# The down projection as seven products per block pair in three parts, its activations stored with their sums, and the weight sums added by GpSimd

## The chip, the core and the metric

The kernel runs on one core of a Trainium2 chip. The core has a matrix engine (TensorE, PE in the tables, with its weight loads as PEld), three engines for elementwise work (VectorE = DVE, ScalarE = ACT, GpSimd = POOL) and a queue engine that only issues transfers (SyncE = SP). Each engine works through its own list of instructions in order and waits at an instruction until the semaphores that it names are set. Sixteen DMA engines move data between the chip's DRAM and the on-chip memory (SBUF); TensorE's results land in PSUM. The metric is the device time of one execution in microseconds (us), lower is better.

## The reference, cut to what matters

One layer of an encoder in float32: an input projection, two attention branches, a gated merge with an output projection, and a convolutional GLU. The change lies in the GLU, and there in its last matrix product above all:

```python
SEQ, D_MODEL, D_FF = 512, 2048, 5632
h2 = rmsnorm(x, norm_ffn)
u  = h2 @ w_up                                   # (512, 2048) @ (2048, 11264)
u  = up[:, :-2]*cw[0] + up[:, 1:-1]*cw[1] + up[:, 2:]*cw[2] + conv_b   # up: u padded by one token
gate, val = jnp.split(u, 2, axis=-1)             # 5632 columns each
x  = x + (jax.nn.silu(gate) * val) @ w_down      # (512, 5632) @ (5632, 2048)
```

## The kernel before, in words

All matrices are held transposed (features on the 128 partitions, the 512 tokens along the free axis). A float32 product is made from three passes: every operand is split into a rounded half `hi` (a cast by ACT) and the rest `lo` (a subtraction by DVE), and hi·hi + hi·lo + lo·hi are summed in PSUM. All TensorE work goes through the helper `mm` (L77), and every SP transfer through `dma` (L74).

The program is a list of steps, run one after the other: attention and gates, the output projection (`project_out`), 22 slices of the up projection (`up`), and the down projection (`down`). A plain step takes weight units of 1024 columns in all (`Plain`: L154 is the cast, L155 the subtraction) and issues 24 matmuls of 128x512 for each.

The up projection is not a plain product. `products` computes a 512x512 block of the result from 2x2 blocks with seven block products in place of eight (Strassen's method in Winograd's form). For this the weights and the activations of a pair of 128-row blocks enter as seven matrices each: four blocks or their sums. A unit there is a `Product`: SP loads four weight blocks of 128x256 (`load`), three added operations make the four sums (`sums`, L573, L576, L577, all on DVE), and `prep` casts and subtracts them in two pieces, of 1024 and 768 columns (L596, L597). TensorE then issues 7 x 2 x 3 = 42 matmuls of 128x256. After the eight products of a slice, `combine` joins the seven PSUM banks into the two results (`u`); four of its DVE operations read PSUM. The activations' seven forms are made once (`forms`).

Each slice ends in a queue of eight entries, one run after each of the next eight products: scale by the row factor (L852), the convolution (`Conv`: ACT makes the three weighted copies, L865, L867, L873, and GpSimd's queue issues two accumulating DMAs for each of gate and val, L868, L875), SiLU (L887), the product with the gate (L890) and the store of the slice's two 128-row blocks to DRAM (`act`, L891, GpSimd's queue).

The order around the change: while TensorE runs product i, `advance` prepares product i+2, forms the sums of product i+3 and loads product i+5. `keep` pins an instruction to its written place on its engine; the rest is placed by the scheduler. For part of the products (in the middle slices the numbers 2, 3 and 7, in the first and last slice all eight; 76 in all) the sums are made much earlier, during gates and `project_out` (`make_early`), stored to DRAM by GpSimd's queue (`sums`, L580), and loaded again in place of the fourth block.

The down projection is plain: two parts of 11 slices each, in each part four steps of 512 output features, 22 units per step: 88 units, 2112 matmuls of 128x512. Its activations are read back from `act` and split once per part (`load_act`, `split_act`, L921, L922). The first part's results are added to x (`total`) in DRAM, the second's to that, and go out (L945, L950).

Of the kernel before, what the change touches and what calls it, by code (L numbers as in the profile page):

```python
# [38 lines left out]
def trunk_kernel(  # L39
# [14 lines left out]
    wst_ctx, att_ctx, f_ctx = ExitStack(), ExitStack(), ExitStack()  # L54
# [117 lines left out]
    def advance(*between):  # L172
# [7 lines left out]
        make_early()  # L180
# [363 lines left out]
    ffn, products_, early, made = {}, [], deque(), deque()  # L544
    keep = tc.keep_in_program_order

    class Product:
# [5 lines left out]
        def __init__(self, w, first, kept, turn):  # L553
            self.w, self.first, self.turn = w, first, turn
            self.kept = dram.tile([P, 4, 256], F32, name=f"sums{first}") if kept else None
            self.made = False

        def ready(self, phase, n):
            return "f" in ffn and not early and self.first <= n

        def load(self):
            f = self.f = ffn["f"].tile([P, 7, 256], F32, tag="f", name="f", bufs=4)
            dma(f[:, 0:2], self.w[:, :, 0])
            dma(f[:, 2], self.w[:, 1, 1])
            if self.made:
                dma(f[:, 3:], self.kept)
            else:
                dma(f[:, 6], self.w[:, 0, 1])

        def sums(self):  # L570
            if not self.made:
                f = self.f
                keep(nc.vector.tensor_tensor(  # L573
                    f[:, 3:5], f[:, 2::-2], f[:, 6].unsqueeze(1).to_broadcast([P, 2, 256]),
                    ALU.add))
                keep(nc.vector.tensor_tensor(f[:, 5], f[:, 4], f[:, 2], ALU.add))  # L576
                keep(nc.vector.tensor_tensor(f[:, 6], f[:, 5], f[:, 1], ALU.add))  # L577

        def store(self):
            nc.gpsimd.dma_start(self.kept, self.f[:, 3:])  # L580
            self.made = True
# [20 lines left out]
    def make_early():  # L602


        if "f" not in ffn or not early:
            return
        made.append(0)
        if len(made) % 5 == 0:
            return
        n = len(made) - len(made) // 5 - 1  # L610
        for move, i in (("store", n - 2), ("sums", n - 1), ("load", n)):
            if 0 <= i < len(early):
                getattr(early[i], move)()
        if n - 2 == len(early) - 1:
            early.clear()

# [3 lines left out]
    def forms(src):  # L620
# [4 lines left out]
        nc.vector.tensor_tensor(  # L625
# [401 lines left out]
```

## Time and profile before

| | |
|---|---|
| time, three runs | 2525.92 us median (2524.97 to 2532.28) |
| profiled execution | 2526.16 us; its span on the core 2524.4 us |
| granted TensorE clock | 0.999 |
| busy: PE, DVE, ACT, POOL | 2510.1, 1514.3, 1120.3, 205.8 us |
| up projection, 1195 to 2040 us | PE 843.6 of 845 us, DVE 683.5, ACT 537.5, POOL 112.0 |
| down projection, 2040 us to the end | PE 480.5 of 484.4 us, DVE 157.6, ACT 120.4, POOL 11.4 |
| read from and written to DRAM | 347.9 and 68.2 MB |

The page of the profile sums each engine's busy time over the span. The chain of waits follows the end of the execution back, at each point to what released the instruction. The view by windows gives the same sums for a stretch of time, with the count of instructions in brackets, the granted clock, the DMA share and GB/s. The timeline lists instructions by start and length (in us); "x2" are two in a row, counted as one stretch, and consecutive operations overlap a little at their ends. In the tables by form a row ends in busy time and mean ns of one.

### The profile page before, as it was taken

The page shows a single profiled execution, that of the slowest core. Times are in us where ns is not written, and L with a number is a line of the kernel's source. Part 1 is how long each engine was busy: PE and PEld are TensorE (multiplying, and loading weights), DVE is VectorE, ACT ScalarE, POOL GpSimd, SP SyncE. Part 2 cuts the span into 40 slices and gives each one's busy share as a digit, 9 for nine tenths or more (in the row PEclk, how much of TensorE's full clock was granted, in tenths as well). Part 3 has the DMA queues.
Part 4 walks back from the last instruction along what each step waited for, and adds up shares of the span by engine and source line. Part 5 has one row for each costly group of instructions (what it writes and reads, how often), then busy time and mean ns, then how long its engine had stood idle before and what let it go on. Part 6 is the DMA issues. An engine that isn't in the chain of part 4 may idle for free.

```text
span 2524.4 us, 38263 instructions
## 1 busy us (share of the span) xinstructions
PE 2510.1 (99%) x15016; PEld 2233.5 (88%) x15016; DVE 1514.3 (60%) x2155; ACT 1120.3 (44%) x1613; POOL 205.8 (8%) x248
## 2 busy tenths in 40 slices
PE   9999999999999999999999999999999999999999
PEld 7888888888888888888999999999999988888887
DVE  6566554635545457646788888888887762243222
ACT  5355544533122232325566666666666662132211
POOL 0100000000000000100011111111111110000000
PEclk9999999999999999999999999999999999999999
DMA  5323232337877887965578788787787895464443
GB/s 189 98 79 92 89 95 90 98 90 242 255 251 248 259 280 242 302 209 169 164 205 222 201 207 213 208 216 203 211 217 204 239 259 167 127 224 132 127 136 106
DMA packets 294677, 464.67 MB, mean 184 GB/s; under 512 B 23136, under 2 KB 190688, under 8 KB 294496
## 3 DMA queue, kind: packets, MB, share of 16 engines
q1 hardware_dynamic: 249408, 348.00, 44.3%
q0 software_dynamic: 40480, 105.83, 16.5%
q10 hardware_dynamic: 4608, 8.39, 0.9%
q8 instruction: 117, 1.92, 0.3%
q14 instruction: 64, 0.52, 0.1%
HBM read 347.93 MB, written 68.16 MB: 165 GB/s over the span
## 4 chain that ended last, share of the span: by engine, by line
PE 97%; DMA 2%; ACT 1%; DVE 0%; issue 0%; SPq 0%; ACTq 0%; DVEq 0%; POOLq 0%
PE mm L77 93%; PE tr L77 2%; PE tr L476 1%; DMA o<-a 1%; DMA s<-act 0%; PE tr L334 0%; ACT wh L596 0%; DMA f<-sums 0%; DVE wl L597 0%; PE tr L383 0%; DMA f<-in_w_up 0%; DMA raw<-in_w_in 0%; ACT s L632 0%; ACT t L248 0%; SPq L74 0%
## 5 line engine op out<-in xcount | busy, mean ns | idle before, releaser
L77 PE MATMUL mm<-s,hi 128*128 128x512 f32 x3712 | 1106.2, 390 | 0.9 <-DVE s L714 0.9
L77 PEld LDWEIGHTS mm<-s,hi 128*128 128x128 f32 x3712 | 695.9, 188 | 144.0 <-ACT s L715 1.3
L77 PE MATMUL mm<-s,wh 128*128 128x256 f32 x4928 | 807.0, 277 | 2.8 <-ACT wh L596 2.5
L155 DVE TENSOR_TENSOR lo<-raw,hi 128x1024 fp32r<-128x1024 f32 (+1 forms) x289 | 352.6, 1220 | 675.1 <-ACT hi L154 663.2
L77 PEld LDWEIGHTS mm<-s,wh 128*128 128x128 f32 x4928 | 701.0, 188 | 3.5 <-ACT wh L596 2.9
L154 ACT CAST hi<-raw 128x1024 fp32r<-128x1024 f32 (+1 forms) x289 | 303.5, 1050 | 879.5 <-PE mm L77 810.6
L77 PE MATMUL mm<-s,lo 128*128 128x512 f32 x1856 | 681.8, 390 | 0.0
L77 PE MATMUL mm<-s,wl 128*128 128x256 f32 x2464 | 583.6, 277 | 1.1 <-DVE wl L597 1.1
L597 DVE TENSOR_TENSOR wl<-f,wh 128x1024 fp32r<-128x1024 f32 x352 | 372.2, 1087 | 141.4 <-ACT wh L596 139.5
L596 ACT CAST wh<-f 128x1024 fp32r<-128x1024 f32 x352 | 317.7, 940 | 281.4 <-PE mm L77 255.0
L77 PEld LDWEIGHTS mm<-s,wl 128*128 128x128 f32 x2464 | 419.0, 188 | 1.5 <-DVE wl L597 1.5
L77 PEld LDWEIGHTS mm<-s,lo 128*128 128x128 f32 x1856 | 348.5, 188 | 71.5
L77 PE MATMUL mm<-hi,s 128*128 128x512 f32 x896 | 285.0, 394 | 5.6 <-ACT hi L154 5.6
L77 PEld LDWEIGHTS mm<-hi,s 128*128 128x128 f32 x896 | 167.8, 189 | 38.4 <-ACT hi L154 5.6
L77 PE MATMUL mm<-lo,s 128*128 128x512 f32 x448 | 176.3, 395 | 0.0
L573 DVE TENSOR_TENSOR f<-f 128x512 f32<-128x512 f32 x176 | 120.4, 684 | 0.0
L77 PEld LDWEIGHTS mm<-lo,s 128*128 128x128 f32 x448 | 84.6, 189 | 16.8
L580 POOL DMA_DIRECT2D sums<-f x76 | 40.6, 534 | 570.2 <-DVE f L577 570.2
L577 DVE TENSOR_TENSOR f<-f 128x256 f32<-128x256 f32 x176 | 74.6, 424 | 5.5
L576 DVE TENSOR_TENSOR f<-f 128x256 f32<-128x256 f32 x176 | 74.6, 424 | 5.3
L875 POOL DMA_DIRECT2D o<-a x44 | 52.6, 1197 | 304.4 <-ACT wh L596 152.0
L865 ACT ACTIVATE o<-u,smalls 128x512 f32<-128x512 f32 x88 | 71.2, 809 | 7.0 <-DVE o L890 4.0
(134 smaller groups left out, 1454.9 us busy)
## 6 DMA issues: line engine op xcount, KB each, us to landing
f<-in_w_up SPq DMA_DIRECT2D x252, 256.0 KB, 3.5
f<-in_w_up SPq DMA_DIRECT2D x428, 128.0 KB, 3.9
raw<-in_w_in SPq DMA_DIRECT2D x103, 512.0 KB, 3.8
raw<-in_w_down SPq DMA_DIRECT2D x88, 512.0 KB, 4.2
o<-a POOLq DMA_DIRECT2D x88, 511.0 KB, 6.2
sums<-f POOLq DMA_DIRECT2D x76, 512.0 KB, 5.1
f<-sums SPq DMA_DIRECT2D x76, 512.0 KB, 5.8
raw<-in_w_in SPq DMA_DIRECT2D x66, 256.0 KB, 3.0
```

What stands on the lines that cost most here:

```text
L77: nc.tensor.matmul(o, l, r, start=start, stop=stop, skip_group_check=True)
L154: nc.scalar.copy(hi[:, c:c + n], self.raw[:, c:c + n])
L155: nc.vector.tensor_tensor(lo[:, c:c + n], self.raw[:, c:c + n], hi[:, c:c + n].bitcast(F32), ALU.subtract)
L476: nc.tensor.transpose(b[:, (j - j0) * P:(j - j0 + 1) * P], pr[j][:, off:off + P], ident)
L573: keep(nc.vector.tensor_tensor(f[:, 3:5], f[:, 2::-2], f[:, 6].unsqueeze(1).to_broadcast([P, 2, 256]), ALU.add))
L576: keep(nc.vector.tensor_tensor(f[:, 5], f[:, 4], f[:, 2], ALU.add))
L577: keep(nc.vector.tensor_tensor(f[:, 6], f[:, 5], f[:, 1], ALU.add))
L580: nc.gpsimd.dma_start(self.kept, self.f[:, 3:])
L596: keep(nc.scalar.copy(hi, f))
L597: keep(nc.vector.tensor_tensor(lo, f, hi.bitcast(F32), ALU.subtract))
L865: keep(nc.scalar.activation(self.o[:, m], u[:, m], AF.Identity, bias=cb[:, i:i + 1], scale=cw[:, i, 1:2]))
L875: nc.gpsimd.dma_start(self.o[:, :, :S - 1], third[:, :, 1:], accum_op=ALU.add)
```

## The change

- `down` uses `products` as `up` does: seven block products per pair of 256 input features. The 22 pairs are taken in three parts of 7, 7 and 8, four steps each. That is 88 products of 42 matmuls of 128x256, 3696 in all.
- `up` makes the three activation sums before it stores (`form_sums`, three DVE operations per slice) and stores eight blocks of 128x256 instead of four, from SP's queue and one queue entry later. The last accumulating DMA of the gate is issued three entries later than before. `down` loads seven of the blocks per pair, and splits them.
- The DRAM copies of weight sums are gone. Each product's sums are made when it is used: by GpSimd in four additions of 128x256, except two of eight products (0 and 5) in slices after the first, and one or two per step in `down`, which stay on DVE with three additions.
- The results of the first two parts are added to `total` by accumulating DMAs from GpSimd's queue; in the third part DVE adds `total`, and the output leaves in two transfers of 512 KB per step.

```diff
-        def ready(self, phase, n):
-            return "f" in ffn and not early and self.first <= n
+        def ready(self, phase, n):
+            return "f" in ffn and self.first <= n
         def load(self):
             f = self.f = ffn["f"].tile([P, 7, 256], F32, tag="f", name="f", bufs=4)
             dma(f[:, 0:2], self.w[:, :, 0])
             dma(f[:, 2], self.w[:, 1, 1])
-            if self.made:
-                dma(f[:, 3:], self.kept)
+            dma(f[:, 6], self.w[:, 0, 1])
+
+        def sums(self):
+            f, add = self.f, lambda *args: keep(self.adder.tensor_tensor(*args, ALU.add))
+            if self.adder is nc.vector:
+                add(f[:, 3:5], f[:, 2::-2], f[:, 6].unsqueeze(1).to_broadcast([P, 2, 256]))
             else:
...
+                add(f[:, 3], f[:, 2], f[:, 6])
+                add(f[:, 4], f[:, 0], f[:, 6])
+            add(f[:, 5], f[:, 4], f[:, 2])
+            add(f[:, 6], f[:, 5], f[:, 1])
...
-    act = [dram.tile([P, 2, S], F32, name=f"act{j}") for j in range(pairs_ff)]
+    act = [dram.tile([P, 8, 256], F32, name=f"act{j}") for j in range(pairs_ff)]
...
+    parts = [range(7), range(7, 14), range(14, pairs_ff)]
...
+    def load_act(part, n):
+        if 0 <= n < len(parts[part]):
+            tiles = [slot(F32R) for _ in range(7)]
+            for o, i in zip(tiles, (0, 2, 7, 5, 4, 6, 3)):
+                dma(o[:, 256:].bitcast(F32), act[parts[part][n]][:, i])
+            acts[part].append(tiles)
+    def split_act(part, n):
+        if 0 <= n < len(parts[part]):
+            for o in acts[part][n]:
+                hi, lo = o[:, :256], o[:, 256:]
+                keep(nc.scalar.copy(hi, lo.bitcast(F32)))
+                keep(nc.vector.tensor_tensor(
+                    lo, lo.bitcast(F32), hi.bitcast(F32), ALU.subtract))
+    def next_part(part, n):
+        load_act(part, n)
+        split_act(part, n - 2)
...
             def out_part():
                 keep(nc.vector.tensor_tensor(v.o, g.o, v.o, ALU.mult))
-                nc.gpsimd.dma_start(act[s], v.o)
+                made.extend(form_sums(v.o))
+            def store():
+                y, one, two = made
+                dma(act[s][:, 0:4], y)
+                dma(act[s][:, 4:6], one)
+                dma(act[s][:, 6:8], two)
+            one, two, three = (unfinished.popleft() for _ in range(3))
             queue.extend((
-                wait, lambda: (before(), scale(gate)), after, lambda: (g.middle(), g.last()),
-                partial(scale, val), v.middle, wait, v.last))
-            unfinished.extend((silu, out_part))
+                wait, lambda: (one(), scale(gate)), two,
+                lambda: (three(), g.middle(), scale(val)), v.middle, wait, g.last, v.last))
+            unfinished.extend((silu, out_part, store))
...
+        def before(i):
+            if n == 0:
+                next_part(part, 7 + i)
...
+            if part < 2 and n == 3:
+                next_part(part + 1, i)
+            if part == 2 and i == 4:
+                for j in range(2):
+                    held.append(quad("ao"[j]))
+                    dma(held[j], total[2 * n + j])
+        def evac(*results):
+            for j, r in enumerate(results):
+                if part < 2:
+                    keep(nc.gpsimd.dma_start(total[2 * n + j], r, accum_op=ALU.add))
+                else:
+                    keep(nc.vector.tensor_tensor(r, r, held[j], ALU.add))
+                    nc.scalar.dma_start(
+                        out.rearrange("(j m p) n -> j p m n", m=2, p=P)[2 * n + j], r)
+        products(view[n], parts[part], acts[part], evac, before=before,
+                 on_vector=(0,) if n in (0, 3) else (0, 3))
```

How the lists of instructions move. GpSimd, one slice in the middle of the up projection, before: five DMA issues and nothing else (`o<-a` are the accumulating DMAs of the convolution, `act` the store).

```order
L868 DMA o<-a 128x2x511
L875 DMA o<-a 128x2x511
L868 DMA o<-a 128x2x511
L875 DMA o<-a 128x2x511
L891 DMA act_138<-o 128x1024
```

GpSimd, the same stretch with the change (L849 and L857 are the accumulating DMAs now, L565 the weight sums in the tile `f`):

```order
L849 DMA o<-a 128x2x511
L565 TENSOR_TENSOR f<-f 128x256 x4
L849 DMA o<-a 128x2x511
L565 TENSOR_TENSOR f<-f 128x256 x4
L857 DMA o<-a 128x2x511
L565 TENSOR_TENSOR f<-f 128x256 x4
L857 DMA o<-a 128x2x511
L565 TENSOR_TENSOR f<-f 128x256 x12
```

Between the four DMA issues of a slice GpSimd now has 24 additions, and the store is gone from its list.

DVE, the last step of a part of the down projection, with the change (from the split of the third product on; `wl` is the weights' lower half, `s` the activations of the next part, L565 the one set of sums that DVE keeps):

```order
L588 TENSOR_TENSOR wl<-f,wh 128x768
L879 TENSOR_TENSOR s<-s 128x256 x7
L588 TENSOR_TENSOR wl<-f,wh 128x1024
L588 TENSOR_TENSOR wl<-f,wh 128x768
L879 TENSOR_TENSOR s<-s 128x256 x7
L588 TENSOR_TENSOR wl<-f,wh 128x1024
L588 TENSOR_TENSOR wl<-f,wh 128x768
L565 TENSOR_TENSOR f<-f 128x512
L565 TENSOR_TENSOR f<-f 128x256 x2
L879 TENSOR_TENSOR s<-s 128x256 x7
```

DVE, at such a place before (the last step of the first part, where the second part's activations are split):

```order
L155 TENSOR_TENSOR lo<-raw,hi 128x1024
L922 TENSOR_TENSOR s<-s 128x512 x2
L155 TENSOR_TENSOR lo<-raw,hi 128x1024
L922 TENSOR_TENSOR s<-s 128x512 x2
L155 TENSOR_TENSOR lo<-raw,hi 128x1024
```

Where two operations on activations stood between two weight units, seven shorter ones stand now, and they come in five of a step's seven products.

DVE, the end of the program, with the change (`mm` is PSUM, L653 and L664 are `combine`, L943 the addition of `total`):

```order
L653 TENSOR_TENSOR t<-t,mm 128x512
L653 TENSOR_TENSOR t<-t,u 128x512
L664 SCALAR_TENSOR_TENSOR t<-mm,t 128x512
L653 TENSOR_TENSOR u<-mm,t 128x2x256
L653 TENSOR_TENSOR u<-t,u 128x1024
L943 TENSOR_TENSOR u<-u,a 128x1024
L943 TENSOR_TENSOR u<-u,o 128x1024
```

Before, the end was `L945 TENSOR_TENSOR u<-mm,u 128x512 x4`, one addition for each of four PSUM banks; now seven operations follow one another, each of the last three on what came before.

More of the change, by code (lines that the diff above doesn't have):

```diff
@@ L600, in prep, with form_sums @@
                 work()
[L602 to L615, printed above, removed]
     def quad(tag):
         return ffn["q"].tile([P, 2, S], F32, tag=tag, name=tag, bufs=2)
-    def forms(src):
+    def form_sums(src):
         y = src.rearrange("p j (t n) -> p (j t) n", t=2)
@@ L635, in forms, with products @@
         return res
[L637 removed]
+    def products(w, pairs, acts, evac, before=None, on_vector=()):
+        n = len(pairs)
         def run():
             ps = []
[L641 removed]
+            for i in range(n):
                 if before:
```

117 lines of the change are left out of this document (36 added, 81 removed).

## The prediction

> **What bounds the kernel now.** I read the page first, then the chain of waits, then windows, then the timeline of single engines.
>
> ```profile
> span 2524.4 us, 38263 instructions
> PE 97%; DMA 2%; ACT 1%; DVE 0%; issue 0%; SPq 0%; ACTq 0%; DVEq 0%; POOLq 0%
> ...
> 1223.92 748.31 PE mm L77 x6568
> ...
> 2036.88 483.62 PE mm L77 x2152
> 2520.52 0.69 DVE u L945
> ```
>
> These are the span, the shares of the chain and its pieces that matter here: TensorE alone sets the end, from 1224 to 1972 us in the up projection and from 2037 us to the last output. So a saving counts where it shortens TensorE's list, and an addition costs where it makes TensorE wait. The pace by windows (columns: stretch, length, then busy us and instructions of PE, PEld, DVE, ACT and POOL, the granted clock, DMA share, GB/s):
>
> ```profile
> 1240.00:1960.00 720.00, 720.00 (x6324) 720.00 (x6324) 589.86 (x749) 459.55 (x601) 100.18 (x93) 1.00 0.80 208
> 2060.00:2500.00 440.00, 440.00 (x1943) 364.34 (x1942) 135.40 (x138) 106.45 (x119) 9.65 (x13) 1.00 0.49 152
> 1438.30:1476.60 38.30, 38.30 (x338) 38.30 (x338) 31.27 (x41) 24.31 (x33) 5.36 (x5) 1.00 0.81 210
> ```
>
> A 128x256 matmul of the up projection takes 720/6324 = 113.85 ns, a 128x512 one of the down projection 440/1943 = 226.45 ns: per column the same, within 0.6%. The period of an up slice comes from one instruction of its queue, 18 slices apart:
>
> ```profile
> 1290.89 0.60 POOL L891 DMA_DIRECT2D act<-o  x1 [17.02 <-DVE o L890]
> 1980.19 0.60 POOL L891 DMA_DIRECT2D act<-o  x1 [14.79 <-DVE o L890]
> ```
>
> 689.30/18 = 38.29 us, 4.79 us per product or 114.0 ns per matmul; I use this one. DVE is busy for 31.27 us of it, the next nearest to the bound.
>
> **What the change takes from TensorE.** Down before: from the last up matmul, about 2041.6, to 2520.5 us, 479 us for 2112 matmuls (226.8 ns). After: 3696 x 114.0 ns = 421.3 us. The gain is **57.7 us**. I add nothing for the more frequent joins of banks: the same joins fall 18 times into the unbroken 748 us above.
>
> **The end of the program.** Now 2524.4 - 2520.5 = 3.9 us follow TensorE: one addition (0.69 us) and 3.2 us until the output has landed. With the change four DVE operations (682 to 692 ns) that end with the last bank, one of 1024 columns, and two more of 1024 for `total` follow one another.
>
> ```profile
> L672 DVE TENSOR_TENSOR u<-mm,t 128x512 f32<-128x512 f32 x44 | 30.0, 682 | 3.4 <-ACT t L675 3.4
> L672 DVE TENSOR_TENSOR u<-t,u 128x1024 f32<-128x1024 f32 x22 | 26.8, 1218 | 0.0
> ```
>
> The last but one bank is done 6 x 0.114 = 0.7 us before the end, so these take 4 x 0.68 - 0.7 + 3 x 1.22 = 5.7 us, plus 3.2: 8.9 in place of 3.9, **+5 us**.
>
> **Weight sums and stores that go.** The 76 early sums lie under gates and output projection, where TensorE runs without a gap; taking them out gains nothing. That they need no second loading relieves DMA in the up projection (896 KB per kept product become 512).
>
> **The GpSimd additions, the dear part.** GpSimd and DVE do not always work side by side. These rows are from the attention stage: the small power operation of GpSimd (L239) and the DVE operations around it.
>
> ```profile
> 482.51 1.01 POOL L239 TENSOR_TENSOR rq<-rq,mhalf 128x4 f32<-128x4 f32 x1 [1.71 <-DVE rq L238]
> ...
> 103.97 4.47 POOL L239 TENSOR_TENSOR rq<-rq,mhalf 128x4 f32<-128x4 f32 x2 [4.75 <-DVE rq L238]
> ...
> 402.57 1.91 POOL L239 TENSOR_TENSOR rq<-rq,mhalf 128x4 f32<-128x4 f32 x1 [0.89 <-DVE rq L238]
> ```
>
> ```profile
> 104.14 0.42 DVE L327 TENSOR_TENSOR qr<-t 128x256 f32<-128x256 f32 x1
> 104.47 0.17 DVE L238 TENSOR_SCALAR rq<-rq 128x4 f32<-128x4 f32 x1
> 104.56 1.21 DVE L155 TENSOR_TENSOR lo<-raw,hi 128x1024 fp32r<-128x1024 f32 x1
> 105.69 0.68 DVE L324 TENSOR_TENSOR t<-qr,masks 128x512 f32<-128x512 f32 x1
> 106.30 0.68 DVE L325 TENSOR_TENSOR t<-qr,masks 128x512 f32<-128x512 f32 x1
> 106.90 0.68 DVE L312 TENSOR_TENSOR qr<-qr,rq 128x512 f32<-128x512 f32 x1
> ...
> 402.40 1.22 DVE L155 TENSOR_TENSOR lo<-raw,hi 128x1024 fp32r<-128x1024 f32 x1
> ```
>
> Undisturbed it takes 1.01 us. The one at 402.57 ends at 404.48, 0.86 us after the DVE operation with two inputs in SBUF that ran when it came (to 403.62). The two at 103.97 end at 108.44, 0.86 us after the last of four such operations in an unbroken row (to 107.58). So GpSimd's reading waits until DVE has none of these in flight, however many follow one another. I take reading as one resource that the two share in turn, though no row shows a DVE operation waiting for GpSimd. The Trainium skill says the same and adds that direction (SBUF — State Buffer, section Who interferes with whom): the later of the two blocks until the earlier ends. These rows agree for GpSimd's side, and no run here shows the other.
>
> What one slice needs of it: DVE's 31.27 us less four `combine` operations that read PSUM (2.7 us), less three of five sets of sums, plus `form_sums`, the same three shapes as a set:
>
> ```profile
> 1440.60 0.68 DVE L573 TENSOR_TENSOR f<-f 128x512 f32<-128x512 f32 x1
> 1441.32 0.43 DVE L576 TENSOR_TENSOR f<-f 128x256 f32<-128x256 f32 x1
> 1441.78 0.42 DVE L577 TENSOR_TENSOR f<-f 128x256 f32<-128x256 f32 x1
> ```
>
> A set is 1.53 us, so 31.3 - 2.7 - 4.6 + 1.5 = **25.5 us**. That leaves 38.3 - 25.5 = 12.8 us for 24 additions, 0.53 us each. No row has such an addition. The nearest:
>
> ```profile
> masks.py:199 POOL TENSOR_SCALAR_AFFINE_SELECT ident<-ident 128x128 f32<-128x128 f32 x1 | 0.3, 284 | 0.0
> L90 POOL MEMSET ones<- 128x128 f32 x1 | 0.2, 207 | 0.0
> L1019 POOL MEMSET const-float32-0.0<- 128x1 f32 x1 | 0.1, 98 | 0.2 <-issue 0.2
> ```
>
> With 98 ns to start, writing costs (207 - 98)/127 = 0.86 ns per column, reading one input and writing 1.46. For 256 columns that is 0.32 us (writing alone, the lower end), 0.47 us (as the one-input operation) and 0.84 us (twice that, the upper end). I take **0.47**, the row that is nearest in kind: it reads a whole tile. Then a slice needs 25.5 + 11.3 = 36.8 of 38.3 us and costs nothing. At 0.84 it would need 45.7. GpSimd's own list is no bound (5.4 us busy in the slice's window, less a store, and 11.3 more), but it is in order: sums that stand behind an accumulating DMA wait for ACT's weighted copies too, and the sums are wanted two products after they are written in the list, 9.6 us, which covers ACT's part of one product.
>
> The Trainium skill has a price of its own (GPSIMD Engine Reference, section Performance versus the Vector engine): 4497 ns for a two-input addition of 2048 columns, scaled 0.56 us for 256, an estimate; by it the sum below comes out within a few us of no change.
>
> **Bursts.** The activations of the next part are split in five products of the last up slice and of each part's last step, and the rest in the step after. One pair is 7 DVE operations of 256 columns, which start 0.34 us apart (104.14 and, with the small one between, 104.56; four in a row of another place below): 2.4 us.
>
> ```profile
> 1199.28 1.42 DVE L633 TENSOR_TENSOR s<-t,s 128x256 fp32r<-128x256 f32 x4
> 1438.59 2.09 DVE L597 TENSOR_TENSOR wl<-f,wh 128x1024 fp32r<-128x1024 f32 x2
> ```
>
> A step of seven products lasts 33.5 us on TensorE, one of eight 38.3. Of shared reading it needs 2.09 us per product for weights, 1.53 per set of sums on DVE, 1.9 for `combine`, 2.4 per pair split, 0.47 per addition. Last up slice: 36.8 + 11.9 = 48.7, over by 10.4. Last steps of the first two parts: 14.6 + 1.5 + 1.9 + 11.9 + 11.3 = 41.2, over by 7.7 each. First steps: 34.1 in 33.5, over by 0.6 in parts one and two, and 42.9 in 38.3, over by 4.6, in part three, which splits three pairs. The middle steps fit (29.0 in 33.5). Weights are prepared about one product ahead, so a burst that starts from a full lead loses 4.8 us less: 5.6 + 2.9 + 2.9 + 0.6 + 0.6 + 4.6 = **17 us**.
>
> DMA in the last slice: eight weight units of 0.52 MB, seven activation loads of 0.92 MB, 1 MB stored and about 4 MB for accumulation are 13.6 MB in 38.3 us, 355 GB/s; the fullest stretch of before had 321:
>
> ```profile
> 2014.90:2041.50 26.60, 25.84 (x226) 25.52 (x225) 19.57 (x24) 22.73 (x34) 4.34 (x5) 1.00 1.06 321
> ```
>
> That would be 4 us more, in the shadow of the 10.4.
>
> **The sum.** 2526.2 (the profiled execution; its span 2524.4 and 1.8 around it) - 57.7 + 5 + 17 = **2490.5 us**, 1.4% faster. The median of the runs shown is 2525.9, 0.2 below that execution, which changes nothing.
>
> **Rivals.**
>
> *Slower: the shared reading decides in the up projection.* One mechanism: an addition above 0.53 us no longer fits into a slice, GpSimd's sums come late, ACT waits for them with the weight cast, and TensorE with the weights. At 0.62 us a slice needs 40.4, 2.1 too much, 42 us over 20 slices; the bursts by the same sums grow to 47 (14 + 2 x 6.5 + 2 x 4.2 + 8.8 + 3). 2526.2 - 57.7 + 5 + 42 + 47 = **2562**. At 0.53 the total is 2500, so above 0.53 each 0.01 us costs 7, and from 0.57 us on the kernel is slower than before. For it: two inputs should cost more than the one of the row I took, and turns between two engines lose something at each. Against it: sums are made a product ahead of their split, and DVE, waiting for ACT, leaves gaps of 1.5 to 2.5 us.
>
> *Faster: the additions hide wholly.* If reading is shared finely rather than by whole operations, only DVE's own time counts: 28.2 us per slice, and 40.1 in the last one, within the lead. 2526.2 - 57.7 + 5 = **2473.5**. Against it stand the seven us at 103.97.
>
> *No change: the store of the activations holds ACT.* `v.middle` writes the tile that the slice before stores, and now stands one product behind the store instead of three. The store waits for DVE, then lands in about what it took before,
>
> ```profile
> act<-o POOLq DMA_DIRECT2D x22, 512.0 KB, 4.2
> ```
>
> and 4.2 of 4.8 us leaves 0.6. A DVE that runs 2.6 us late in the products after `combine` makes ACT, and all behind it, wait 2 us per slice: 2490.5 + 42 = **2532**. Against it: the casts of that product stand ahead of `v.middle`, 1.8 us more.
>
> **How the numbers follow.** Forecast 0.38, wholly hidden 0.20, reading decides 0.32, store 0.10. The forecast's own range is 2478 to 2512 (0.43 to 0.55 us per addition). The range reaches from the second case to somewhat beyond the first rival's figure: 2470 to 2575; what an addition near the upper end would give, above 2700, is left out. A measurement of this kernel tells about 0.3%, 7.6 us, from no change. Faster: the forecast and the hidden case and a little of the third, 0.60. Same: 0.09. Slower: 0.31.
>
> **What would show it.** Right: the chain of waits again over 96% TensorE; 3696 matmuls of 128x256 in about 440 us after the up projection; the period of a slice 38.3 us; GpSimd's additions at 0.4 to 0.5 us in DVE's gaps; the waits that remain lie in the last up slice and around each part's last step. Wrong: a period of 40 us and more with ACT's casts released by `f` of GpSimd (the first rival); additions over DVE operations at their full speed (the second); ACT's L865 wait released by DMA of `act` (the third). The forecast also fails if 256-column matmuls slow down in `down`, or if the end after the last matmul is far from 9 us.

## The result

The changed kernel takes **2696.36 us** (median of four, 2694.09 to 2698.51), the kernel before on the same chip 2526.16 us (2524.97 to 2532.28). The ratio is 1.067, 95% interval 1.065 to 1.069: **170 us slower**. The forecast was 2490.5 us with a range of 2470 to 2575; the time lies 121 us above the range.

The head of the page of the profile after:

```profile
span 2696.7 us, 43019 instructions
PE 2534.8 (94%) x16600; PEld 2313.2 (86%) x16600; DVE 1873.2 (69%) x2119; ACT 1240.4 (46%) x1847; POOL 1113.4 (41%) x974
```

TensorE was busy for 2510.1 of 2524.4 us before. It now issues fewer columns and is yet busy for longer, and 162 us of the span lie outside its busy time. The stretches of the up projection (its steady part on), of the down projection and of one middle slice, by windows (columns as in the prediction):

```profile
1195.00:2183.40 988.40, 897.41 (x7403) 876.84 (x7402) 866.20 (x778) 549.30 (x730) 712.03 (x608) 0.97 0.63 164
2183.40:2687.30 503.90, 451.66 (x3699) 443.94 (x3697) 428.56 (x451) 229.87 (x357) 346.48 (x300) 0.95 0.58 160
1605.52:1650.37 44.85, 41.15 (x336) 40.21 (x336) 39.29 (x35) 24.60 (x33) 32.59 (x29) 0.96 0.64 165
```

- The last matmul of the up projection is at 2183.4 us in place of 2041.6: **+141.8**. From SiLU to SiLU a middle slice lasts 45.1 us (44.8 in the mean) in place of 38.3. By the first matmuls of the slices, the 20 middle ones add 123 us, the first slice 9 (51.9 in place of 42.6) and the last one 9 (49.1 in place of 40.3).
- The down projection takes 503.9 us up to its last matmul, in place of 478.9: **+25.0**, where 421.3 was forecast.
- After the last matmul come 9.4 us (2687.3 to 2696.7) in place of 3.9: **+5.5**.

Together 172.3 us, the whole difference of the spans (2696.7 - 2524.4).

In the middle slice DVE is busy for 39.29 us, where TensorE alone needs 38.3 and DVE's undisturbed operations would take 28.2 (25.5 and 2.7 of the prediction's account). So DVE is held up for 11.1 us, 0.46 for each of the 24 additions in the mean, and stands idle for the other 5.6 us of the slice. GpSimd is busy for 32.59 us and waits at its DMA issues for 11 more, so its list is full too. What the waits say (engine and line, what released it, total us, times, longest):

```profile
ACT wh L587 <- POOL f L565: 357.3, 140, 9.6
...
POOL o L849 <- ACT a L848: 172.5, 40, 11.5
DVE wl L588 <- ACT wh L587: 171.5, 137, 3.3
...
PE mm L77 <- DVE wl L588: 116.4, 96, 6.7
```

From the top: ACT's weight cast waits for GpSimd's sums, GpSimd at its accumulating DMAs for ACT's copies, DVE for ACT, TensorE for DVE. Before, the chain of waits of the whole program was 97% TensorE; now TensorE waits 96 times for the lower half of the weights, 116.4 us in all.

The groups by form that carry it (busy us, mean ns of one):

```profile
L565 POOL TENSOR_TENSOR f<-f 128x256 f32<-128x256 f32 x816 | 990.7, 1265 | 113.5 <-DMA f<-in_w_up 36.6 <-DMA f<-in_w_down 33.2 <-DVE wl L588 6.7
L588 DVE TENSOR_TENSOR wl<-f,wh 128x1024 fp32r<-128x1024 f32 x264 | 397.4, 1505 | 112.8 <-ACT wh L587 111.3 <-DMA f<-in_w_down 0.7 <-DMA f<-in_w_up 0.5
L653 DVE TENSOR_TENSOR u<-mm,t 128x512 f32<-128x512 f32 x68 | 46.2, 680 | 4.6 <-PE mm L77 4.4
```

A GpSimd addition takes 1.27 us in the mean, where 0.47 was assumed. The DVE operation of 128x1024 with both inputs in SBUF takes 1.51 us in place of 1.22; the one that reads PSUM takes 680 ns, as before. So the two engines hold each other up, and only where DVE reads two inputs from SBUF. The timelines show how, GpSimd's four additions of one set against DVE's list:

```profile
1608.95 6.23 POOL L565 TENSOR_TENSOR f<-f 128x256 f32<-128x256 f32 x4
```

```profile
1609.72 1.75 DVE L833 TENSOR_TENSOR u<-u,row 128x1024 f32<-128x1024 f32 x1
1611.40 3.18 DVE L588 TENSOR_TENSOR wl<-f,wh 128x1024 fp32r<-128x1024 f32 x2
1614.51 1.75 DVE L896 TENSOR_TENSOR o<-o 128x1024 f32<-128x1024 f32 x1
```

Each DVE operation has let one addition in: 1.75 in place of 1.22 us, 0.53 to 0.54 us longer, and the additions come at the pace of DVE's operations. Of the 816 additions 52 met no DVE operation; their median is 0.74 us (0.72 to 1.05). The other 764 take 1.30 us in the mean. So an addition costs 0.74 us alone, takes 1.3 in turns, and holds DVE up by 0.54 when they meet.

A second loss lies behind the gaps that this leaves on TensorE. One gap of 2.31 us, and the stretches of 1.5 us around it:

```profile
1626.71 0.39 PE L77 MATMUL mm<-s,wl 128*128 128x256 f32 x1 [2.31 <-DVE wl L588]
```

```profile
1626.00:1627.50 1.50, 0.79 (x6) 0.80 (x7) 1.50 (x2) 1.50 (x3) 0.00 (x0) 1.00 0.14 40
1627.50:1629.00 1.50, 1.50 (x10) 1.50 (x9) 0.02 (x1) 1.50 (x3) 0.41 (x1) 0.54 0.15 27
1629.00:1630.50 1.50, 1.50 (x9) 1.50 (x9) 1.24 (x2) 0.97 (x2) 1.50 (x2) 0.50 0.82 266
1630.50:1632.00 1.50, 1.50 (x13) 1.50 (x12) 1.41 (x2) 0.87 (x1) 1.50 (x2) 0.82 1.05 216
1632.00:1633.50 1.50, 1.50 (x16) 1.50 (x15) 1.29 (x1) 0.18 (x1) 1.42 (x2) 1.00 1.10 199
```

After the gap the granted clock is one half for 3.4 us, and 9 or 10 matmuls fall into a stretch, where 16 do at the full clock. There are 27 such intervals (3.41 us or multiples, the last cut off by the end of the program), 108.6 us in all; before there were two, 5.0 us. By the mean granted clock

```profile
core 0: 2696.7 us, clock 0.980
```

they are worth about 50 us of TensorE's time (0.020 x 2534.8); before it was 0.999.

Which gaps are followed by it can be read from the same trace. A gap of 2.3 to 2.7 us comes once in each of 20 slices, from 1310 to 2165 us. After 13 of them the clock was halved, after 7 it was not, as here:

```profile
1447.61 0.39 PE L77 MATMUL mm<-s,wl 128*128 128x256 f32 x1 [2.32 <-DVE wl L588]
```

```profile
1447.60:1451.00 3.40, 3.39 (x29) 3.39 (x30) 1.65 (x2) 3.28 (x5) 1.49 (x2) 1.00 0.36 115
```

All 27 intervals begin on one grid of 3.413 us (those at 1583.26, 1627.63 and 1672.01 are 13 steps apart each). In the 13 cases at least 1.82 us of the gap lay within one step of this grid, and the step behind it is the one at half the clock. In the 7 cases the edge of a step cut the gap, and at most 1.76 us lay within one: the gap above falls into parts of 1.44 and 0.88.

### The profile page after: what moved, and what is told of

It reads as the page before. It is cut to its first block, busy times and chain, and to the rows that moved or that the text cites. A ratio compares the mean times of both kernels' runs of the same rounds, so it can differ in the third digit from the quotient of the medians.

```text
span 2696.7 us, 43019 instructions
## 1 busy us (share of the span) xinstructions
PE 2534.8 (94%) x16600; PEld 2313.2 (86%) x16600; DVE 1873.2 (69%) x2119; ACT 1240.4 (46%) x1847; POOL 1113.4 (41%) x974
## 3 DMA queue, kind: packets, MB, share of 16 engines
q0 software_dynamic: 27520, 58.64, 11.6%
## 5 line engine op out<-in xcount | busy, mean ns | idle before, releaser
L77 PE MATMUL mm<-s,wh 128*128 128x256 f32 x7392 | 1300.8, 283 | 29.4 <-ACT wh L587 25.0
L77 PEld LDWEIGHTS mm<-s,wh 128*128 128x128 f32 x7392 | 1132.3, 193 | 37.2 <-ACT wh L587 29.0
L77 PE MATMUL mm<-s,wl 128*128 128x256 f32 x3696 | 1013.6, 285 | 116.5 <-DVE wl L588 116.4
L565 POOL TENSOR_TENSOR f<-f 128x256 f32<-128x256 f32 x816 | 990.7, 1265 | 113.5 <-DMA f<-in_w_up 36.6
L588 DVE TENSOR_TENSOR wl<-f,wh 128x1024 fp32r<-128x1024 f32 (+1 forms) x528 | 704.4, 1364 | 180.1 <-ACT wh L587 171.5
L77 PEld LDWEIGHTS mm<-s,wl 128*128 128x128 f32 x3696 | 696.1, 193 | 137.1 <-DVE wl L588 136.8
L587 ACT CAST wh<-f 128x1024 fp32r<-128x1024 f32 (+1 forms) x528 | 487.9, 942 | 675.5 <-POOL f L565 357.3
L77 PE MATMUL mm<-s,hi 128*128 128x512 f32 x2304 | 689.7, 390 | 0.9 <-DVE s L695 0.9
L77 PEld LDWEIGHTS mm<-s,hi 128*128 128x128 f32 x2304 | 431.7, 188 | 89.4 <-ACT s L696 1.3
L77 PE MATMUL mm<-s,lo 128*128 128x512 f32 x1152 | 425.0, 390 | 0.0
L565 DVE TENSOR_TENSOR f<-f 128x512 f32<-128x512 f32 x180 | 203.8, 1132 | 4.1
L77 PEld LDWEIGHTS mm<-hi,s 128*128 128x128 f32 x896 | 167.9, 189 | 38.5 <-ACT hi L154 5.7
L849 POOL DMA_DIRECT2D o<-a x44 | 52.9, 1202 | 181.2 <-ACT a L848 172.5
```

The costliest lines, as they stand in the source:

```text
L77: nc.tensor.matmul(o, l, r, start=start, stop=stop, skip_group_check=True)
L565: f, add = self.f, lambda *args: keep(self.adder.tensor_tensor(*args, ALU.add))
L587: keep(nc.scalar.copy(hi, f))
L588: keep(nc.vector.tensor_tensor(lo, f, hi.bitcast(F32), ALU.subtract))
L849: keep(nc.gpsimd.dma_start(self.o[:, :, 1:], first[:, :, :S - 1], accum_op=ALU.add))
```

## The experiments

Two theories stood at the start. **Shared reading:** DVE and GpSimd take turns at reading SBUF; each addition takes longer than assumed and holds DVE up, and the sum of the two passes TensorE's 38.3 us. **Something else that the change moved:** the store and the later accumulating DMAs, the crowded steps of the down projection, or GpSimd's order, which puts sums behind DMA issues that wait for ACT. The first five runs take the additions, the down projection and the store apart; the others ask what of the loss a better order or division gives back.

**The sums on DVE.** Everything of the change but the engine:

```diff
-                w[pairs[i]], len(units), nc.vector if i in on_vector else nc.gpsimd, i == 0)
+                w[pairs[i]], len(units), nc.vector, i == 0)
```

> The changed kernel with all weight sums on DVE (three additions per product, as in the kernel before), none on GpSimd; all else as changed. Theory A (DVE and GpSimd take turns at reading SBUF, and that makes the weights late): DVE operations return to their lengths of before (1.22 us for 128x1024 against 1.76), a slice of the up projection falls from 45.0 to 38.3 to 39 us although DVE has more to do (about 37.4 of 38.3 us), down keeps most of its gain: 2480 to 2520 us. Theory B (the loss comes from the other parts: the later store, the seven act splits, 256-column matmuls in down): the slice stays above 42 us and the time above 2600.

Measured: 2541.25 us, 1.0061 of before (1.0046 to 1.0076): 155 of the 170 us are gone, though the time lies above the 2480 to 2520 that was expected. A window of some ten slices:

```profile
1600.00:2000.00 400.00, 391.66 (x3411) 389.70 (x3411) 379.30 (x529) 245.79 (x321) 48.03 (x40) 1.00 0.73 187
```

A slice lasts 39.4 us, somewhat above the 38.3 to 39 expected, of which DVE is busy for 37.4 (379.30/400). That is the undisturbed sum, 28.2 + 6 x 1.53 = 37.4, and the 128x1024 operation is back at 1223 ns. The loss hangs on GpSimd making the sums. A set costs DVE 1.53 us if DVE adds it, and up to 4 x 0.54 = 2.16 us of being held up if GpSimd does.

**GpSimd's sums without the rest.** The kernel before, with no sums kept in DRAM, sums by GpSimd except products 0 and 5, and the plain down projection:

```diff
-            u = Product(v[i, :, :, :, c:c + 256], len(units), i in kept, i == 0)
+            u = Product(v[i, :, :, :, c:c + 256], len(units), nc.vector if i in on_vector else nc.gpsimd, i == 0)
...
-                 kept=range(8) if s in (0, pairs_ff - 1) else (2, 3, 7))
+                 on_vector=(0, 5) if s else ())
```

> The kernel before, with its plain down projection and its stores, but with the weight sums as in the changed kernel (GpSimd, products 0 and 5 on DVE, none kept in DRAM). Theory A: the slice is as long as in the changed kernel, 43 to 45 us, 2526 + 21 x 6 = about 2650 us (2620 to 2680). Theory B: within 20 us of the kernel before.

Measured: 2703.07 us, 1.0700 (1.0684 to 1.0716), a slice of 46.4 to 47.3 us. The sums alone make the whole loss. The expectation missed the size; why the slice is 1.3 to 2.2 us longer here than in the changed kernel was not pursued (the old order has the activations' store in GpSimd's list too, and its accumulating DMAs at other places). The additions are as slow as with the whole change:

```profile
L570 POOL TENSOR_TENSOR f<-f 128x256 f32<-128x256 f32 x536 | 631.5, 1245 | 48.5 <-DMA f<-in_w_up 21.2 <-DVE s L629 6.3
```

**The down projection without GpSimd's sums.** The new down projection, `form_sums` and the new store, with the up projection's sums kept in DRAM as before, and the down projection's all on DVE:

```diff
-        products(view[:, :, :, :, s * 256:(s + 1) * 256], range(KD // 2), h2, evac,
-                 before=before, on_vector=(0, 5) if s else ())
+        products(view[:, :, :, :, s * 256:(s + 1) * 256], range(KD // 2), h2, evac,
+                 before=before, kept=range(8) if s in (0, pairs_ff - 1) else (2, 3, 7))
...
-                 on_vector=(0,) if n in (0, 3) else (0, 3))
+                 kept=())
```

> Down as seven products with activations stored as their sums, but the up projection's weight sums as in the kernel before (76 kept in DRAM, the rest on DVE) and those of down on DVE. Theory A: no slice longer than 38.3 us, 57.7 us less TensorE work in down, less some 15 to 25 us where DVE has sums and act splits in the same products: 2485 to 2505 us. Theory B: above 2600 us.

Measured: 2516.84 us, 0.9964 (0.9950 to 0.9978): **faster than before**, though by less than expected. The middle slices have their 38.3 us. The first row is its down projection, the second a stretch of the up projection:

```profile
2052.00:2505.70 453.70, 432.00 (x3699) 427.14 (x3697) 417.06 (x653) 224.31 (x349) 18.75 (x21) 0.99 0.64 180
1600.00:2000.00 400.00, 400.00 (x3512) 400.00 (x3511) 344.97 (x448) 260.97 (x337) 51.61 (x43) 1.00 0.86 226
```

The up projection ends at 2052.0 us, 10.4 later than before, 6.5 of it in the last slice (46.8 us in place of 40.3) and most of the rest in the first; the down projection takes 453.7 us, DVE busy for 417.06 of them. So seven products are worth 25 us here (478.9 - 453.7), and the later end of the up projection and the end of the program take 16 of that back.

**GpSimd writes in place of adding.** The four additions become four constant writes of the same size at the same places; this leaves the weight sums of the products that GpSimd handles out:

```diff
-                add(f[:, 3], f[:, 2], f[:, 6])
-                add(f[:, 4], f[:, 0], f[:, 6])
+                for i in (3, 4, 5, 6):
+                    keep(nc.gpsimd.memset(f[:, i], 1.0))
+                return
```

> The changed kernel with every GpSimd addition replaced by a GpSimd fill of the same 128x256 block (the weight sums are left out, so the products are not the reference's). GpSimd keeps its places in the order and its writes, but reads nothing. Theory A (reading is what is shared): DVE at its undisturbed lengths, slice 38.3 us, some 2480 to 2500 us. Rival (GpSimd's list in order, its DMA issues and waits, or its writing, make the sums late): slice above 42 us, above 2600 us.

Measured: 2492.89 us, as expected for shared reading. This run and the next five, up to the two changes of order together, are single executions; they differ from the changed kernel by 38 us and more. The groups, then the down projection and a stretch of the up projection:

```profile
L589 DVE TENSOR_TENSOR wl<-f,wh 128x1024 fp32r<-128x1024 f32 x264 | 322.9, 1223 | 224.1 <-ACT wh L588 191.1 <-DMA f<-in_w_up 19.9 <-DMA f<-in_w_down 11.1
L570 POOL MEMSET f<- 128x256 f32 x816 | 262.2, 638 | 275.1 <-DMA f<-in_w_down 157.9 <-DMA f<-in_w_up 63.5 <-DVE wl L589 42.3
```

```profile
2042.80:2481.90 439.10, 426.73 (x3699) 424.40 (x3697) 320.49 (x444) 232.10 (x357) 94.25 (x298) 0.99 0.67 189
1600.00:2000.00 400.00, 400.00 (x3516) 400.00 (x3515) 301.47 (x355) 260.58 (x337) 119.02 (x295) 1.00 0.76 194
```

816 instructions of GpSimd stand in the same list, behind the same DMA issues, with the same store and the same later accumulating DMAs, and nothing is lost in the middle slices of the up projection: a slice takes 38.3 us, DVE's operation 1223 ns. So the store, the moved DMAs and the crowded steps are not the loss (the last cost 18 us in the down projection), and the 204 us between this run and the changed kernel are what the additions cost over writes. A write is also shorter than an addition, 0.64 against 1.27 us in the mean, so this run alone does not part GpSimd's reading from its time. Each addition costs the end 0.26 us in the up projection ((2183.4 - 2042.8)/536) and 0.23 in the down projection ((503.9 - 439.1)/280).

**One input in place of two.** As before, but the four additions are copies of one block to another (the sums are left out too):

```diff
+                for i, j in ((3, 2), (4, 0), (5, 4), (6, 5)):
+                    keep(nc.gpsimd.tensor_copy(f[:, i], f[:, j]))
+                return
```

> The changed kernel with every GpSimd addition replaced by a GpSimd copy of one block (the sums are left out, the products are not the reference's): the same 24 operations per slice at the same places, one input instead of two. If the time for which an operation reads is what costs, the copy (0.47 us by the forecast's row, so about half the reading) lets the slice fall from 45.0 to 38.5 to 41 us and the time to 2495 to 2560 us. If it is the count of turns between the engines, each GpSimd operation waiting for a whole DVE operation, the slice stays above 42.5 us and the time above 2620 us.

Measured: 2506.49 us, within the range expected if reading time is what costs, and a slice of 38.3 us. So it is not the count of turns: 24 operations at the same places cost the slice nothing. All copies of the line (minimum, median and maximum in ns), then DVE's group:

```profile
L570 POOL COPY f<-f x816: 396/591/3310, 1161.0 to 2478.1; 128x256 f32<-128x256 f32 x164
```

```profile
L589 DVE TENSOR_TENSOR wl<-f,wh 128x1024 fp32r<-128x1024 f32 x264 | 340.2, 1289 | 187.9 <-ACT wh L588 164.6 <-DMA f<-in_w_up 22.1 <-DMA f<-in_w_down 0.5
```

A one-input operation of this size takes 0.40 us at the least and lengthens DVE's by 66 ns in the mean. The prediction's 0.47 was not far off for what its row was, one input; the second input makes 0.72 at the least of it and raises DVE's lengthening from 66 to 282 ns.

**Five of eight products' sums on DVE.** Half of the up projection's GpSimd sums go over:

```diff
-                 before=before, on_vector=(0, 5) if s else ())
+                 before=before, on_vector=(0, 1, 4, 5, 6) if s else ())
```

> The changed kernel with the sums of five of eight products on DVE in the up projection (0, 1, 4, 5, 6) and three on GpSimd, 12 additions per slice in place of 24; down unchanged. Taking turns costs for each addition: about half the loss of a slice, 45.0 to some 41 to 42 us, 2696 - 20 x 3.3 = about 2630 us (2600 to 2660). If a fixed thing in the slice (the later store, the order of the DMA issues) made the loss, it stays at 44 to 45 us.

Measured: 2596.27 us, just under what was expected, a slice of 39.8 us in place of 41 to 42.

```profile
1700.00:2060.00 360.00, 349.61 (x3044) 347.77 (x3043) 349.66 (x390) 224.41 (x295) 152.03 (x145) 1.00 0.74 188
```

DVE is busy for as long as TensorE, 97%. The prediction's account of a slice, with one price put in for 0.47, fits both: with 24 additions 25.5 + 24 x 0.81 = 44.9 (45.0 to 45.1 measured, from which the price is taken), with 12 of them and three more sets on DVE 25.5 + 3 x 1.53 + 12 x 0.81 = 39.8. So the effective price of an addition is **0.81 us**, somewhat above its 0.74 alone. It is not the time for which an addition reads: of the 0.81, 0.46 is DVE held up, and lateness and the halved clock are in the rest. Nor does the account cover every slice: with no addition on GpSimd it gives 25.5 + 6 x 1.53 = 34.7 us, less than TensorE's 38.3, where 39.4 was measured. There DVE's whole list takes 37.4 us, with the four operations that read PSUM, which the account leaves out; that this list came too near to 38.3 is the likely reason, not a tested one.

**The order.** Is part of the price that sums come late? GpSimd stands at its accumulating DMAs until ACT's copies are there, and the sums behind have to wait:

```profile
1619.40 1.20 POOL L849 DMA_DIRECT2D o<-a  x1 [4.22 <-ACT a L848]
...
1628.59 1.20 POOL L849 DMA_DIRECT2D o<-a  x1 [4.50 <-ACT a L848]
...
1637.41 1.20 POOL L857 DMA_DIRECT2D o<-a  x1 [2.40 <-ACT a L855]
```

These 11.1 us of a slice can be filled in two ways: sums one product earlier, or the accumulating DMAs one queue entry later (after the copies they wait for), and both.

```diff
-        for phase, d in (("sums", 2), ("load", 4)):
+        for phase, d in (("sums", 3), ("load", 4)):
```

> The changed kernel with each product's sums written into the lists one product earlier (the phase distance 3 in place of 2), the same operations otherwise. If the loss is lateness (the sums are there too late for a fixed chain sums, cast, subtraction), one product more of lead takes most of it: slice 38.5 to 41 us, below 2600 us. If it is the two engines' capacity while they take turns, the slice stays at 44 to 45 us, within 30 us of 2696.

```diff
+            self.first = first
+
+        def middle_add(self):
             keep(nc.gpsimd.dma_start(
-                self.o[:, :, 1:], first[:, :, :S - 1], accum_op=ALU.add))
+                self.o[:, :, 1:], self.first[:, :, :S - 1], accum_op=ALU.add))
...
             queue.extend((
-                wait, lambda: (one(), scale(gate)), two,
-                lambda: (three(), g.middle(), scale(val)), v.middle, wait, g.last, v.last))
+                zero, lambda: (one(), scale(gate)), two,
+                lambda: (three(), g.middle(), scale(val)),
+                lambda: (g.middle_add(), v.middle()), v.middle_add, g.last,
+                lambda: (g.last_add(), v.last())))
```

> The changed kernel with the four accumulating DMAs of each slice issued one product later than the copies they add, so that GpSimd, which works in order, no longer stands at an issue waiting for ACT (about 11 us of each slice in the changed kernel, 33 us busy). If GpSimd's list is the bound of a slice through these waits, the slice falls from 45.0 to 40.5 to 42.5 us and the time to 2590 to 2650 us. If the loss is the turns alone (DVE held up by 24 additions, 0.54 us each), the waits move elsewhere and the slice stays at 44 to 45 us.

> Both: the issues one product later and the sums one product earlier. What is left is the capacity that the two engines share: 25.5 us of DVE operations with two inputs in SBUF, 2.7 us that read PSUM and 24 x 0.54 us are 41.2 us per slice. Turns: slice 41 to 42.5 us, 2590 to 2640 us. If it falls to 38.3 us, lateness was all, and shared reading no bound.

Measured: 2645.79 us with a slice of 43.4 (sums earlier), 2658.42 us with slices of 40.9 to 45.2, in the mean 43 (DMAs later), 2649.2 us with slices of 41.0 to 45.1, in the mean 43.4 (both). Each gives some 2 us per slice and 38 to 51 us of the 170, and both together no more than one. No run fell within a range that was written down for it: the first two slices lie between the values for lateness and those for turns, the third lies above both. GpSimd's waits between 1700 and 2060 us, of the changed kernel and with the DMAs later:

```profile
POOL o L849 <- ACT a L848: 67.4, 16, 4.5
POOL o L857 <- ACT a L855: 19.6, 8, 2.7
```

```profile
POOL f L565 <- DMA f<-in_w_up: 40.2, 20, 4.7
POOL o L852 <- ACT a L848: 38.8, 12, 5.0
```

87.0 us at issues have become 38.8, and GpSimd waits 40.2 for weights instead. The expectation that the slice would come down with the waits was wrong: these two ways of taking lateness out give back at most 2 of the 6.8 us. What holds the rest is not settled by them. Between 1700 and 2060 us of the run with both, DVE is busy for 86% and GpSimd for 72%, so neither list is full, and the granted clock is 0.96.

**The version that gains, with more sums kept.** The third run with the sums of products 2, 4 and 6 also kept for three steps of the down projection in which activations are split; to make room for them, early sums are formed after seven of eight units of gates and output projection in place of four of five:

```diff
-                 kept=())
+                 kept=(2, 4, 6) if (part, n) in ((0, 3), (1, 3), (2, 0)) else ())
```

> The kernel with down alone changed (2516.8 us), and three products of each of the three crowded steps of down (the last step of the first two parts, the first of the third) with sums kept in DRAM too, 85 in place of 76, made in seven of eight preparation calls in place of four of five. DVE has 4.6 us less to do in each of these steps: 2503 to 2513 us. If the weights' transfers rather than DVE limit these steps, no gain: 2515 to 2525.

Measured: 2514.11 us (2510.41 to 2517.49), 0.9953 (0.9938 to 0.9967). Faster than before by 0.5%, just above the range expected; from the third run it cannot be told apart. DVE's sums in the crowded steps are at most a small part of what keeps these two from the 421 us of the down projection. Where the loss lies shows in the third run's steps, each taken from its first matmul to the next step's: the last steps of the first two parts, where two thirds of the newly kept sums are, lose only 0.5 us each, and the first steps of the three parts 8.2, 8.6 and 9.7 of 31.7 us in all (42.2 us, say, where TensorE needs 33.5). With more sums kept, those first steps still lose 10.0, 6.3 and 9.4. What they wait for was not parted.

## Why the prediction was wrong

**What bounds the kernel, and what the change takes from TensorE: right.** With writes in place of the additions the up projection ends at 2042.8 us and the down projection takes 439.1, which is 421.3 plus 18. The 57.7 us were there to be had. (The old down projection has 11 weight units per step, not 22; the 88 units and 2112 matmuls are right.)

**The end of the program: right.** 9.4 us, against 8.9; seven DVE operations follow one another from 2686.63 to 2692.84.

**Weight sums and stores that go: right in what was said,** nothing before the up projection got faster. But the first slice, whose sums had all been kept, now lasts 51.9 us in place of 42.6, and 45.5 even with writes, for which the prediction has no term. And kept sums had a worth that this step did not price: 76 sets that cost DVE nothing in the up projection. That is why the run with kept sums and the new down projection gains, and the run with all sums on DVE (39.4 us per slice) doesn't.

**The GpSimd additions: the step that failed, by its price.** "I take 0.47, the row that is nearest in kind: it reads a whole tile." The row has one input; an addition has two. The copy run shows the row's kind, 0.40 us at the least; the addition takes 0.72 us at the least, near the upper end of 0.84 that the prediction itself had worked out from "twice that". The path that the first rival names is the one in the rows: sums late, ACT's cast waiting for them, TensorE for the weights. The prediction's own formula, 2500 us and 7 per 0.01 us above 0.53, gives 2500 + 28 x 7 = 2696 at 0.81, where 2696 was measured. The 0.81 is itself taken from the slice, and since the bursts were sized too small (below), that it comes out to the microsecond is luck. So the first rival happened, at a price that the range left out in words: "what an addition near the upper end would give, above 2700". The range's upper end was set by that omission, not by a row.

The step had two further gaps. It weighed only what the two engines share, 25.5 us, against the slice. DVE's own list is 28.2 us, and whatever the additions hold DVE up by comes on top of that: 39.3 us were busy, more than TensorE's 38.3. And it had a row only for GpSimd waiting for DVE. The other direction, cited then from the Trainium skill (SBUF — State Buffer, section Who interferes with whom), is now in the rows: DVE's 1.22 us become 1.75 when an addition comes ahead. The rows do not bear out "however many follow one another": at 1609 us each DVE operation let one addition in, though at 2206 us one waited for 8.97. That a DVE operation with one input in SBUF keeps out of it, and that GpSimd's pure writes don't disturb, is in the same section, and agrees with 680 ns for the PSUM reader and 1223 ns in the run with writes. And the estimate by the Trainium skill's other page (GPSIMD Engine Reference, section Performance versus the Vector engine), 0.56 us, is below the 0.72 to 0.74 measured alone. Scaling down from 2048 columns shrinks any fixed part of an instruction along with the rest; that this is the reason is not shown, as no run has another length. The measurement decides.

**GpSimd's own list: wrong by the same price.** "No bound": 5.4 + 11.3 us were forecast, 32.6 were busy and 11 spent waiting for ACT. It was as full as the slice is long.

**The bursts: too small, and not in their place.** 17 us were forecast with additions at 0.47. The copy run, whose operations take 0.40 us at the least, is the nearest to that: its down projection takes 28 us more than 421.3, where 11.6 of the 17 were forecast, and its last up slice, forecast to lose 5.6, takes 38.5 us. With writes the down projection takes 17.8 us more; that run's time of 2492.89 is near the forecast, but its GpSimd operations read nothing, so it does not bear the 17 out. Its last steps of the parts lose nothing; the first steps lose 8.6, 2.3 and 3.5 us and the second of the first part 2.7. With the additions at their real price the down projection loses 82.6 us against 421.3. (The DMA of the last slice is added up wrongly: its four items make 15.6 MB, not 13.6. No term of the sum hangs on it.)

**The rivals.** "The additions hide wholly" fell: DVE's operations of 128x1024 with two SBUF inputs grew from 1.22 to 1.51 us in the mean. (The "seven us at 103.97" that were held against it are 4.47 in their row.) "The store holds ACT" fell: the runs that have the same store, with writes or copies in place of additions, have slices of 38.3 us, and L846 (L865 before), `v.middle`'s cast, never waited for a DMA of `act`. What the first rival did not name is the halved clock after TensorE's gaps, some 50 us of TensorE's time.

**What stays open.** A middle slice is 6.8 us longer. TensorE idles for 3.7 (44.85 - 41.15) and is busy for 2.9 longer (41.15 - 38.3), of which the clock of 0.96 makes 1.8; the last 1.1 lies within what the modelled ends of matmuls allow and is not resolved. How much of the idle 3.7 a slower clock brought on, by letting no lead build up, was not tried. Nor is it settled how much of the 6.8 us is DVE held up and how much is sums that come late because GpSimd itself is slow; the swaps of the additions take both away together. A set of sums with fewer GpSimd instructions was not tried.

## What to carry to other kernels

Price a helper engine by what it takes from the engine beside which it works: here a set of four small GpSimd additions held DVE up by as much as 2.16 us, and DVE makes the same set in 1.53. When a term of the sum decides (7 us per 0.01), take its price from a row with the same number of inputs, or give the upper bound its full chance in the range. A product that saves TensorE's time pays only while the engines that prepare it have room: of 57.7 us, 9 to 12 were kept by the version that leaves the sums in DRAM.

## What the runs showed of the hardware

- A GpSimd addition of 128x256 with two inputs in SBUF takes 0.72 us at the least and 0.74 in the median beside an idle DVE; beside a busy one 1.3 us, and DVE's operations with two SBUF inputs grow by 0.53 to 0.54 us for each that comes between. A copy takes 0.40 us at the least and lengthens them by 0.07 in the mean; a write does not at all.
- The turns are not fair. Behind a DVE list without gaps one addition took 8.97 us. The first of the four additions in this row is the one, and the second fence is DVE's list at that time:

```profile
2206.47 11.89 POOL L565 TENSOR_TENSOR f<-f 128x256 f32<-128x256 f32 x4 [5.34 <-DMA f<-in_w_down]
```

```profile
2206.12 2.09 DVE L588 TENSOR_TENSOR wl<-f,wh 128x1024 fp32r<-128x1024 f32 x2
2208.13 1.22 DVE L833 TENSOR_TENSOR u<-u,row 128x1024 f32<-128x1024 f32 x1
2209.26 2.44 DVE L879 TENSOR_TENSOR s<-s 128x256 fp32r<-128x256 f32 x7
2211.61 2.09 DVE L588 TENSOR_TENSOR wl<-f,wh 128x1024 fp32r<-128x1024 f32 x2
2213.62 1.22 DVE L896 TENSOR_TENSOR o<-o 128x1024 f32<-128x1024 f32 x1
```

  DVE's operations have their undisturbed lengths there; GpSimd got its turn only after them. Why the operations at 1609 us, in a list without gaps too, let one addition in each and these did not, the rows don't tell.
- A gap of TensorE of 2.3 us was followed by 3.4 us at half the granted clock where at least 1.82 us of it lay within one step of a grid of 3.413 us, and not where the grid cut it into parts of at most 1.76. A gap of 2.17 us in the down projection of the run with kept sums was cut into 1.12 and 1.05 and was not followed; one of 2.17 us that lay within one step, in the run with all sums on DVE, was. The border lies at some 1.8 us: at 2656.6 us of the changed kernel 1.84 us within one step were not followed. So one and the same gap was followed by a further loss of 1.7 us (half of 3.41) in one slice and by none in another.
